# Differential heads: the rotation of queries and keys wholly on GpSimd, their squares on ScalarE, the chain of steps spread over two ticks more

## The chip, the core and the metric

The kernel runs on one core of a Trainium2 chip. Five engines work side by side, each through its own queue in order: TensorE (PE in the profile; its weight loads are PEld), VectorE (DVE), ScalarE (ACT), GpSimd (POOL) and SyncE (SP), which here issues nearly all DMAs. An instruction waits on semaphores for what other engines or DMAs must have done first, and all that stands behind it on its queue waits with it. The metric is the device time of one execution in microseconds (us), lower is better.

## What is computed

A decoder layer for 2048 tokens of width 1024. One input projection feeds two groups of attention heads: eight "stick-breaking" heads and four "differential" heads. The differential part is what this case is about; its queries and keys are normalised per 64-wide map and rotated before the attention:

```
def rmsnorm(x, g, eps=NORM_EPS):
    y = xf * lax.rsqrt(jnp.mean(xf * xf, axis=-1, keepdims=True) + eps) * g
def rope(x, pos):
    x1, x2 = xf[..., :half], xf[..., half:]
    return jnp.concatenate([x1 * cos - x2 * sin, x1 * sin + x2 * cos], axis=-1)
...
dq = rope(rmsnorm(to_pair(d_q), diff_q_norm_g[layer]), pos)
dk = rope(rmsnorm(to_pair(d_k), diff_k_norm_g[layer]), pos)
d_out = differential_attention(dq, dk, dv, lam)      # softmax(q1k1) - lam * softmax(q2k2), times v
d_out = rmsnorm(d_out, diff_subln_g[layer], SUBLN_EPS) * (1.0 - lambda_init)
mix = jnp.concatenate([sb_out, d_out], axis=-1)
x = x + mix @ w_o[layer]
x = x + (jax.nn.silu(h2 @ w_gate) * (h2 @ w_up)) @ w_down      # h2 = rmsnorm(x)
```

## The kernel before

Numbers are kept as pairs of float16 (a high part and the rest), so a product is two or three matmuls. Four stages follow one another: the input norm (to some 85 us), attention in eight groups (0 to 3 stick-breaking, a pair of heads each; 4 to 7 differential, one head each), the rest of the output projection, and the feed-forward part.

The attention of the differential groups is cut into units: 128 queries (one of 16 rows `i`) against up to 1024 keys, for one of the two maps (`units_diff`, L878). A group has 48 units. TensorE makes the scores, VectorE takes their maximum (L917), ScalarE makes a bias of it (L925) and the exponentials (L931); once a row's two maps are there, VectorE subtracts one from the other (`mix`, L965), both halves are split off (L974 to L987), transposed by DMA (L327) and multiplied with the values (`values`, L992). The row's norm takes two GpSimd instructions (L1016, and L108 called from there) and then ScalarE (L1024) and VectorE (L1029).

The program's order is made by a clock of **ticks** (`Ticks`, L33). One unit is one tick; `clock.at(d, fn)` puts a step into the tick that is `d` later. So the tick numbers set only the order in which instructions stand in each engine's queue; there is no time in them. Between units TensorE gets pieces of other work: the projections of the next group's queries, keys and values (`project_diff`, L599; one piece per unit), in the last group the first half of the output projection (`output_sb`, L1062; two pieces per unit). When a group's units are over and pieces are left, they are put out alone, a tick each (L1225; for the last group L1261).

Each differential group has four chunks of 512 tokens, 16 chunks in all. After a chunk's queries and keys are projected into the tile `st` (two buffers, `staged` counts those in use), a **chain** of steps runs over it, started by `begin` (L726); only one chain runs at a time, since the tile `rt` has one buffer and `roping` guards it:

- tick 0: `squares` on GpSimd (L663, 128x1024, from `st` into `rt`); tick 1: `rstd`, sums on VectorE (L667, L669), the power on GpSimd (L108)
- tick 3: `normalise` for queries and for keys, VectorE (L675) and GpSimd (L677); ticks 4 and 5: `rotate`, of each half four products and a difference and a sum
- tick 7: `high`; tick 8: `low`, then `finish` with three DMA transposes from `rt`, `rt` and `st` into `k` and `q` (L712). There `st` and, at once, `roping` are given free.

The next chain writes its squares into `rt`, so it has to wait for the DMAs that read `rt`.

## Time and profile before

| what | us |
|---|---|
| median of three runs | 2873.72 |
| the three runs | 2872.24, 2873.72, 2876.29 |
| the profiled execution, its own time | 2869.62 |
| its span in the profile | 2867.8 |
| TensorE, VectorE, ScalarE, GpSimd busy | 2540.9, 2333.7, 1533.4, 1462.7 |
| mean granted TensorE clock | 0.952 of full speed |

The profiled execution took 4.1 us less than the median, and 1.8 us of its time lie outside the span. The first chain of the differential heads begins at 659.6 us (while the last stick-breaking group still runs), and the last one ends at 1332.4 us; after 1340 us nothing of the changed code runs. Busy time counts an instruction from its start to its end, also where it stands still within that time. The chain that ended last follows the work back from the last instruction and tells which engine and line each moment of the span hung on.

### The profile page before, as it was taken

To read this page: it belongs to the slowest core of one execution; us is meant where nothing else is said; L and a number is where in the kernel's file an instruction comes from. 1 tells how busy PE (TensorE), PEld (TensorE's weight loads), DVE (VectorE), ACT (ScalarE), POOL (GpSimd) and SP (SyncE) were. 2 spreads that over 40 slices of the span, in tenths; PEclk is the share of its full clock that TensorE was granted. 3 is DMA by queue.
4 is the path that set the end of the run, shared out by engine and by line. 5 is a ranking of instruction groups with operands and counts; after the bars stand their busy time and mean duration, and the time that the engine had idled before them with its cause. 6 is when DMAs were issued, how large, how long until landed. Compare 5 with 4: busy or idle time off the path is not lost.

```text
span 2867.8 us, 50589 instructions
## 1 busy us (share of the span) xinstructions
PE 2540.9 (89%) x19628; PEld 1470.6 (51%) x19628; DVE 2333.7 (81%) x3639; ACT 1533.4 (53%) x2587; POOL 1462.7 (51%) x1131
## 2 busy tenths in 40 slices
PE   6978888887786887877998989999999999999999
PEld 4534445455675775765853444444444444444444
DVE  7798998988898898998748789889787767776776
ACT  5788788886555655555426544544443433343332
POOL 1454555547667576774214656654444444444542
PEclk8989999998998999988999999999999999999999
DMA  4576888766554556668765222221217421112111
GB/s 159 91 146 120 144 142 142 135 133 122 100 91 91 97 105 109 136 116 178 167 162 130 88 100 74 74 77 60 88 45 147 153 97 45 45 44 89 45 45 74
DMA packets 734242, 301.57 MB, mean 105 GB/s; under 512 B 618672, under 2 KB 713264, under 8 KB 734000
## 3 DMA queue, kind: packets, MB, share of 16 engines
q1 hardware_dynamic: 733856, 298.30, 46.5%
q8 instruction: 153, 2.51, 0.4%
q14 instruction: 89, 0.73, 0.1%
q0 software_dynamic: 144, 0.03, 0.0%
HBM read 127.34 MB, written 28.31 MB: 54 GB/s over the span
## 4 chain that ended last, share of the span: by engine, by line
PE 43%; DVE 20%; ACT 6%; POOL 5%; DMA 5%; issue 5%; SPq 1%; DVEq 0%; POOLq 0%; ACTq 0%
PE pw L167 33%; PE psum L167 10%; DMA wt<-wh 2%; DVE mx L178 2%; DVE fs L1382 2%; DVE acc_a L1655 2%; DVE pp L178 1%; DVE hh L1434 1%; DVE pp L807 1%; DVE wh L836 1%; DMA q<-rt 1%; DVE wmx L105 1%; DVE rt L683 1%; DVE st L675 1%; ACT pp L802 1%
## 5 line engine op out<-in xcount | busy, mean ns | idle before, releaser
L167 PE MATMUL pw<-t,fs 128*128 128x512 f16 x3696 | 806.5, 380 | 9.6 <-ACT fs L1381 3.8
L167 PEld LDWEIGHTS <-fs 128*128 128x128 f16 x3696 | 360.4, 98 | 447.0 <-issue 9.3
L818 POOL TENSOR_TENSOR pp<-pp 128x1024 f32<-128x1024 f32 (+1 forms) x160 | 325.1, 2032 | 316.2 <-DVE pp L815 139.8
L167 PE MATMUL pw<-acc_b,at 128*128 128x512 f16 x2112 | 467.6, 382 | 17.9 <-DVE cg L1580 8.2
L167 PE MATMUL psum<-k,q 64*128 64x512 f16 (+4 forms) x1600 | 290.3, 378 | 157.9 <-DVE pp L810 77.0
L167 PE MATMUL psum<-ws,h_hi 128*128 128x128 f16 x4096 | 379.0, 225 | 20.6 <-ACT psum L1011 11.4
L167 PE MATMUL psum<-ws,h_lo 128*128 128x128 f16 x2048 | 368.2, 224 | 0.0
L167 PEld LDWEIGHTS <-h_hi 128*128 128x128 f16 x4096 | 329.0, 101 | 49.5 <-issue 38.1
L167 PEld LDWEIGHTS <-at 128*128 128x128 f16 x2112 | 206.9, 98 | 270.8 <-issue 28.3
L1583 POOL TENSOR_TENSOR cg<-cg,cu 128x512 f32<-128x512 f32 x88 | 112.1, 1274 | 360.9 <-ACT cg L1582 341.4
L1655 DVE SCALAR_TENSOR_TENSOR acc_a<-pw,isd,acc_a 128x512 f32<-128x512 f32 x352 | 248.7, 745 | 51.1 <-PE pw L167 50.7
L1381 ACT ACTIVATE fs<-acc_b,fst 128x512 f16<-128x512 f32 x264 | 175.9, 713 | 211.3 <-POOL acc_b L1370 145.2
L1382 DVE SCALAR_TENSOR_TENSOR fs<-acc_b,fst,fs 128x512 f16<-128x512 f32 x264 | 248.6, 982 | 33.1 <-ACT fs L1381 33.0
L1572 POOL TENSOR_TENSOR sc<-sc 128x512 f32<-128x512 f32 x132 | 219.4, 1679 | 88.3 <-ACT sc L1566 88.3
L807 DVE TENSOR_TENSOR_SCAN pp<-pp,psum 128x256 f32<-128x256 f32 (+1 forms) x320 | 195.9, 653 | 56.0 <-ACT psum L804 55.1
L167 PEld LDWEIGHTS <-q 64*128 64x128 f16 (+1 forms) x1600 | 95.6, 99 | 269.6 <-issue 113.4
L1566 ACT COPY sc<-pw 128x512 f32<-128x512 f32 x176 | 100.3, 581 | 209.6 <-PE pw L167 186.1
L167 PEld LDWEIGHTS <-h_lo 128*128 128x128 f16 x2048 | 206.9, 101 | 0.0
L836 DVE TENSOR_TENSOR wh<-pp,wh 128x1024 f16<-128x1024 f32 (+1 forms) x160 | 204.7, 1279 | 0.3 <-DMA wt<-wh 0.3
L931 ACT ACTIVATE pp<-psum,nb,ds_sc 128x1024 f32<-128x1024 f32 (+4 forms) x192 | 183.0, 954 | 22.8 <-DVE pp L178 8.6
L178 DVE TENSOR_REDUCE mx<-psum 128x1 f32<-128x1024 f32 (+4 forms) x192 | 173.7, 905 | 20.3 <-PE psum L167 19.5
L802 ACT ACTIVATE pp<-psum,gsc 128x1024 f32<-128x1024 f32 (+1 forms) x160 | 164.8, 1030 | 34.5 <-PE psum L167 30.5
(224 smaller groups left out, 4545.7 us busy)
## 6 DMA issues: line engine op xcount, KB each, us to landing
acc_b<-in_w_gate_dram SPq DMA_DIRECT2D x22, 1024.0 KB, 5.2
acc_b<-in_w_up_dram SPq DMA_DIRECT2D x22, 1024.0 KB, 7.7
acc_b<-in_w_down_dram SPq DMA_DIRECT2D x22, 1024.0 KB, 9.6
raw<-in_w_in_dram SPq DMA_DIRECT2D x24, 512.0 KB, 4.4
pp<-in_x_dram SPq DMA_DIRECT2D x16, 512.0 KB, 5.3
wt<-wh SPq DMA_TRANSPOSE x512, 3.2
raw<-in_w_o_dram SPq DMA_DIRECT2D x16, 512.0 KB, 4.1
mt<-mix_d SPq DMA_DIRECT2D x32, 256.0 KB, 3.3
```

The costliest lines, as they stand in the source:

```text
L167: nc.tensor.matmul(ps, lhsT=lhsT, rhs=rhs, start=start, stop=stop)
L178: fn(*a, **k)
L802: nc.scalar.activation(be, z[:, :, 0:W], AF.Sigmoid, scale=sc[:, 0:1])
L807: nc.vector.tensor_tensor_scan(ga, ga, z[:, h, P:W][:, ::-1], 2.0 ** 14 if diag else cx[a][:, h, 0:1], ALU.mult, ALU.mult)
L818: nc.gpsimd.tensor_mul(b4, b4, gp[:, :, 1:P + 1].rearrange("p h (r n) -> p h r n", r=1).to_broadcast([128, 2, 2, P]))
L836: nc.vector.tensor_sub(wl[:, 0:n], b2, u["wh"][:, 0:n])
L931: nc.scalar.activation(pt, u["z"][:, 0:e - b], AF.Exp, scale=ds_sc, bias=nb[:, m:m + 1], accum_out=su[:, jj:jj + 1])
L1381: nc.scalar.activation(w[:, m, 0:4], src, AF.Copy, scale=sw)
L1382: nc.vector.scalar_tensor_tensor(w[:, m, 4:8], src, sw, w[:, m, 0:4], ALU.mult, ALU.subtract)
L1572: nc.gpsimd.tensor_add(s[m], s[m], y[m])
L1583: nc.gpsimd.tensor_mul(g, g, u)
L1655: nc.vector.scalar_tensor_tensor(acc[:, i, hs], ps, pr.isd, acc[:, i, hs], ALU.mult, ALU.add)
```

## The change

- `squares` moves from GpSimd (a product of `st` with itself) to ScalarE (its Square function), same tile and size.
- `rotate` has no VectorE instruction any more. Before, of the four products of each half VectorE made two (L683, L684; 128x256) and GpSimd two. Now GpSimd makes all, three instructions instead of four: the two sine products of 128x256, and one cosine product of 128x512 in place of the two of 128x256. The difference and the sum stay on GpSimd.
- `high`, `low` and `finish` stand one tick later, and `roping` is given free two ticks after `finish` instead of in it. A chain can so begin at the earliest eleven ticks after the one before, not eight.

```
-                nc.gpsimd.tensor_mul(r["tmp"]...., x3, x3)
+                nc.scalar.activation(r["tmp"]...., st...., AF.Square)
...
-                nc.gpsimd.tensor_mul(y1, x2, bc(1))
-                nc.vector.tensor_mul(y2, x1, bc(1))
-                nc.vector.tensor_mul(x1, x1, bc(0))
-                nc.gpsimd.tensor_mul(x2, x2, bc(0))
+                x = st[:, t].rearrange("p j m (h f) -> p j (m h) f", h=2)
+                nc.gpsimd.tensor_mul(y1, x2, bc(1, 2))
+                nc.gpsimd.tensor_mul(y2, x1, bc(1, 2))
+                nc.gpsimd.tensor_mul(x, x, bc(0, 4))
                 nc.gpsimd.tensor_sub(x1, x1, y1)
                 nc.gpsimd.tensor_add(x2, x2, y2)
...
                 staged[0] -= 1
-                roping[0] = False
+
+                def over():
+                    roping[0] = False
+
+
+                clock.at(2, over)
...
-                clock.at(7, high)
-                clock.at(8, low)
-                clock.at(8, finish)
+                clock.at(8, high)
+                clock.at(9, low)
+                clock.at(9, finish)
```

Line numbers of the changed kernel are one higher from L667 on and six higher from the end of `finish` on. What it does to the queues, at three places:

VectorE's queue in the first chunk of group 7, from the sums on to the two rotations. `mx` is a unit's maximum, `cf` and `pp` belong to `mix`, `st` and `rt` to the chain. Before:

```order
L675 TENSOR_TENSOR st<-st,qss 128x512 x2
...
L952 TENSOR_SCALAR cf<-cf,su,nlam 128x1
L683 TENSOR_TENSOR rt<-st,cs 128x8x32
L684 TENSOR_TENSOR st<-st,cs 128x8x32
L178 TENSOR_REDUCE mx<-psum 128x1
L919 TENSOR_TENSOR mx<-mx 128x1
L683 TENSOR_TENSOR rt<-st,cs 128x8x32
L684 TENSOR_TENSOR st<-st,cs 128x8x32
L178 SCALAR_TENSOR_TENSOR pp<-pp,cf 128x512
L178 TENSOR_REDUCE mx<-psum 128x1
```

Now:

```order
L676 TENSOR_TENSOR st<-st,qss 128x512 x2
...
L958 TENSOR_SCALAR cf<-cf,su,nlam 128x1
L178 TENSOR_REDUCE mx<-psum 128x1
L925 TENSOR_TENSOR mx<-mx 128x1
L178 SCALAR_TENSOR_TENSOR pp<-pp,cf 128x512
L178 TENSOR_REDUCE mx<-psum 128x1
```

The four products of the chain are gone from between the units' own instructions, which keep their order.

GpSimd's queue in the same chunk, the first of the two rotations with what stands around it; `wh` is the low part of a row's weights, `cf` and `oss` belong to rows' norms. Before:

```order
L677 TENSOR_TENSOR st<-st,qkg 128x512 x2
L985 TENSOR_TENSOR wh<-pp,wh 128x1024
L682 TENSOR_TENSOR rt<-st,cs 128x8x32
L685 TENSOR_TENSOR st<-st,cs 128x8x32
L686 TENSOR_TENSOR st<-st,rt 128x8x32
L687 TENSOR_TENSOR st<-st,rt 128x8x32
L956 TENSOR_SCALAR cf<-su,gsc 128x1
L1016 TENSOR_SCALAR oss<-oss,cf 128x1
L108 TENSOR_TENSOR oss<-oss,mhalf 128x1
```

Now:

```order
L678 TENSOR_TENSOR st<-st,qkg 128x512 x2
L991 TENSOR_TENSOR wh<-pp,wh 128x1024
L684 TENSOR_TENSOR rt<-st,cs 128x8x32
L685 TENSOR_TENSOR rt<-st,cs 128x8x32
L686 TENSOR_TENSOR st<-st,cs 128x512
L687 TENSOR_TENSOR st<-st,rt 128x8x32
L688 TENSOR_TENSOR st<-st,rt 128x8x32
L962 TENSOR_SCALAR cf<-su,gsc 128x1
L1022 TENSOR_SCALAR oss<-oss,cf 128x1
L108 TENSOR_TENSOR oss<-oss,mhalf 128x1
```

One product more stands ahead of the rows' norms, and the cosine product is twice as wide.

ScalarE's queue at the start of group 7, around the group's fourth unit, where the chain of its third chunk now begins; `nb` and `pp,su` are a unit's bias and exponentials. Before:

```order
L526 ACTIVATE ws<-raw,wo_sc 128x1024
L925 ACTIVATE nb<-mx,lnk,nds_sc 128x1
L931 ACTIVATE pp,su<-psum,nb,ds_sc 128x256
L1024 ACTIVATE mxs<-on,oss 128x128
L974 CAST wh<-pp 128x1024
```

Now:

```order
L526 ACTIVATE ws<-raw,wo_sc 128x1024
L663 ACTIVATE rt<-st 128x1024
L931 ACTIVATE nb<-mx,lnk,nds_sc 128x1
L937 ACTIVATE pp,su<-psum,nb,ds_sc 128x256
L1030 ACTIVATE mxs<-on,oss 128x128
L980 CAST wh<-pp 128x1024
```

The squares stand ahead of the unit's bias and exponentials.

TensorE's queue moves a little too. The third chunk of group 4 is projected one unit later, so that two ticks of pieces more are put out alone between groups 3 and 4 (six ticks, before four); between the last scores of group 3 and the first of group 4 stand 48 projection matmuls more. And the output projection of the last group starts one unit later: after the last scores 264 of its matmuls are left, before 240.

## Rows read from the trace of the kernel before

**Rows 1.** The page's part 4: the whole chain that ended last, by line.

```profile
PE pw L167 33%; PE psum L167 10%; DMA wt<-wh 2%; DVE mx L178 2%; DVE fs L1382 2%; DVE acc_a L1655 2%; DVE pp L178 1%; DVE hh L1434 1%; DVE pp L807 1%; DVE wh L836 1%; DMA q<-rt 1%; DVE wmx L105 1%; DVE rt L683 1%; DVE st L675 1%; ACT pp L802 1%
```

**Rows 2.** Two stretches: length, then busy PE, PEld, DVE, ACT, POOL, clock, DMA share, GB/s.

```profile
660.00:1340.00 680.00, 517.68 (x6579) 429.41 (x6577) 608.39 (x1010) 382.61 (x880) 463.79 (x434) 0.89 0.60 110
1340.00:1460.00 120.00, 114.11 (x1114) 95.68 (x1114) 79.04 (x143) 49.37 (x104) 24.32 (x29) 1.00 0.78 174
```

**Rows 3.** Sums over 16 chains (L663 to L718), and 16 rotations alone (L683 to L687).

```profile
sum 511.40, PE 374.47 PEld 310.25 DVE 475.18 ACT 284.90 POOL 405.31; mean PE 23.40 PEld 19.39 DVE 29.70 ACT 17.81 POOL 25.33
...
sum 165.00, PE 120.42 PEld 101.43 DVE 162.66 ACT 83.40 POOL 157.44; mean PE 7.53 PEld 6.34 DVE 10.17 ACT 5.21 POOL 9.84
```

**Rows 4.** VectorE's groups, 660 to 1340 us: count | busy us, mean ns | idle before.

```profile
L683 DVE TENSOR_TENSOR rt<-st,cs 128x256 f32<-128x256 f32 x32 | 27.5, 858 | 2.3 <-POOL st L677 2.3
L684 DVE TENSOR_TENSOR st<-st,cs 128x256 f32<-128x256 f32 x32 | 26.6, 832 | 1.1
```

**Rows 5.** Single lines on VectorE: duration in ns, least/median/most, first and last start.

```profile
L683 DVE TENSOR_TENSOR rt<-st,cs x32: 409/417/2404, 677.9 to 1319.9; 128x256 f32<-128x256 f32 x32
...
L684 DVE TENSOR_TENSOR st<-st,cs x32: 424/830/2239, 678.3 to 1320.4; 128x256 f32<-128x256 f32 x32
...
L644 DVE SCALAR_TENSOR_TENSOR v<-psum,v x32: 424/424/426, 636.8 to 1296.4; 128x256 f16<-128x256 f32 x32
```

**Rows 6.** GpSimd's groups, 660 to 1340 us.

```profile
L677 POOL TENSOR_TENSOR st<-st,qkg 128x512 f32<-128x512 f32 x32 | 44.9, 1422 | 7.8 <-DVE st L675 7.8
...
L687 POOL TENSOR_TENSOR st<-st,rt 128x256 f32<-128x256 f32 x32 | 34.3, 1071 | 0.0
...
L663 POOL TENSOR_TENSOR rt<-st 128x1024 f32<-128x1024 f32 x16 | 33.4, 2087 | 26.3 <-DMA q<-rt 26.3
L686 POOL TENSOR_TENSOR st<-st,rt 128x256 f32<-128x256 f32 x32 | 30.4, 949 | 1.5 <-DVE st L684 1.5
L685 POOL TENSOR_TENSOR st<-st,cs 128x256 f32<-128x256 f32 x32 | 27.6, 863 | 2.5
L682 POOL TENSOR_TENSOR rt<-st,cs 128x256 f32<-128x256 f32 x32 | 27.1, 847 | 0.0
```

**Rows 7.** ScalarE's groups, 660 to 1340 us.

```profile
L925 ACT ACTIVATE nb<-mx,lnk,nds_sc 128x1 f32<-128x1 f32 x117 | 44.7, 382 | 109.0 <-DVE mx L919 86.9 <-DVE mx L178 21.9
...
L802 ACT ACTIVATE pp<-psum,gsc 128x1024 f32<-128x1024 f32 x14 | 15.6, 1111 | 1.7 <-PE psum L167 1.6
```

**Rows 8.** Who waited for whom, 660 to 1340 us: us in total, times, longest.

```profile
PE psum L167 <- ACT pp L931: 76.8, 54, 5.6
...
POOL rt L663 <- DMA q<-rt: 26.3, 8, 6.4
...
DVE qss L667 <- POOL rt L663: 17.2, 7, 5.5
...
ACT st L627 <- DMA q<-st: 16.4, 4, 5.7
...
ACT mxs L1024 <- POOL oss L108: 8.5, 7, 3.4
```

**Rows 9.** The chain that ended last, 660 to 1340 us, by line (cut where the view cuts).

```profile
by line: PE psum L167 14.6%; issue 11.0%; DVE mx L178 8.1%; DVE pp L178 5.4%; DMA wt<-wh 4.8%; DMA q<-rt 3.3%; DVE rt L683 3.2%; DVE st L675 2.9%; POOL rt L663 2.3%; DVE wh L178 2.3%; POOL wh L985 2.2%; POOL cf L956 1.9%; SPq L712 1.8%; DVE
```

**Rows 10.** GpSimd in order of time at the start of group 6: start, us, instruction [idle before].

```profile
1082.68 0.66 POOL L718 COPY st<-rt 128x512 f16<-128x512 f16 x1 [0.83 <-DVE rt L709]
1087.32 2.35 POOL L663 TENSOR_TENSOR rt<-st 128x1024 f32<-128x1024 f32 x1 [3.98 <-DMA q<-rt]
```

**Rows 11.** The chain's three transposes (L712), from issue to landing.

```profile
DMA to landing us min/median/max: 3.2/3.5/5.2
```

**Rows 12.** The exponentials of all 192 differential units: durations, first and last start.

```profile
L931 ACT ACTIVATE pp<-psum,nb,ds_sc x192: 437/1042/1208, 750.6 to 1422.8; 128x1024 f32<-128x1024 f32 x80, 128x128 f32<-128x128 f32 x16, 128x256 f32<-128x256 f32 x16, 128x384 f32<-128x384 f32 x16
```

**Rows 13.** The stretch between groups 3 and 4, columns as in rows 2.

```profile
725.00:750.00 25.00, 15.39 (x189) 12.97 (x187) 24.02 (x32) 9.41 (x14) 16.17 (x14) 0.86 0.83 141
```

**Rows 14.** TensorE's groups, 1340 to 1460 us: the first half of the output projection.

```profile
L167 PE MATMUL psum<-ws,mt 128*128 128x256 f16 x720 | 82.9, 272 | 4.6 <-DVE acc_a L1101 2.4 <-DVE acc_b L1101 2.1
```

More of the change, by code (lines that the diff above doesn't have):

```diff
@@ L648, in project_diff, with bc @@
             r = {}
-            def bc(n):
+            def bc(n, k):
                 return r["cs"][:, n].rearrange("p j (o f) -> p j o f", o=1).to_broadcast(
-                    [128, 4, 2, 32])
+                    [128, 4, k, 32])
             x3 = st.rearrange("p t j m d -> p (t j m) d")
@@ L662, in squares @@
                 r["tmp"] = r["rt"][:, 0:1024].rearrange("p (t j m d) -> p t j m d", t=2, j=4, m=2)
-                nc.gpsimd.tensor_mul(r["tmp"].rearrange("p t j m d -> p (t j m) d"), x3, x3)
+                nc.scalar.activation(r["tmp"].rearrange("p t j m d -> p (t j m d)"),
+                                     st.rearrange("p t j m d -> p (t j m d)"), AF.Square)
             def rstd():
@@ L674, in normalise @@
                 y = x3[:, 8 * t:8 * t + 8, :]
-                (nc.vector, nc.vector)[t].tensor_mul(y, y, r["ss"][:, 8 * t:8 * t + 8].rearrange(
+                nc.vector.tensor_mul(y, y, r["ss"][:, 8 * t:8 * t + 8].rearrange(
                     "p (a o) -> p a o", o=1).to_broadcast([128, 8, 64]))
```

## The prediction

> **What bounds the kernel now.** I read the chain that ended last first. For 33% of the span it hangs on TensorE's matmuls into `pw`, which are those of the feed-forward part, where none of the changed code runs; only for 10% on those into `psum`, attention and projections [rows 1]. So I went to the stretch from 660 to 1340 us, which holds all 16 chains. There VectorE is busy 608.4 of 680 us (89%), TensorE 517.7 (76%), GpSimd 463.8 (68%) and ScalarE 382.6 (56%); behind it, from 1340 to 1460, TensorE is busy 114.1 of 120 and VectorE 79.0 [rows 2]. The first stretch is VectorE's, the second TensorE's. Inside the chains it is plainer: their 16 stretches sum to 511.4 us with VectorE busy 475.2 (93%), and in the 165.0 us of the rotations alone VectorE is busy 162.7 and GpSimd 157.4: both are full, and each holds the other up [rows 3].
>
> How they hold each other up shows in single instructions. A rotation product on VectorE takes 409 ns at its least and up to 2404; the median of the second is 830, twice its least of 424 [rows 5]. The 64 of them are busy 27.5 + 26.6 = 54.1 us [rows 4], while at their least they would take 32 x 0.409 + 32 x 0.424 = 26.7. So 27.4 us are standing still inside the instruction. An instruction of the same size on VectorE that reads one operand from PSUM takes 424 to 426 ns in all 32 cases [rows 5], though GpSimd runs beside it too. So it is two SBUF operands that meet GpSimd.
>
> The waits tell who is late: ScalarE stood 86.9 us for VectorE's maxima before the bias [rows 7], TensorE 76.8 us for ScalarE's exponentials, which free the score banks [rows 8]. A late VectorE thus reaches TensorE through ScalarE. The chain that ended last goes through the first rotation product for 3.2% of 680 us, 21.8 us, through the second for less than the list's last entry, 1.8%, or 12 us, and through GpSimd's squares for 2.3%, 15.6 us [rows 9].
>
> **The change, part by part.** The sum is made against the profiled execution's own time, 2869.6 us; the median of the runs, 2873.7, is 4.1 higher, and I add that at the end.
>
> *Rotation off VectorE.* Removed are 64 instructions, 54.1 us busy [rows 4]. All of it counts if VectorE is the bound wherever they stand; the 93% busy inside the chains [rows 3] speaks for nearly all. The chain that ended last gives 21.8 us [rows 9] as the least: another path is then next, mostly the maxima, which VectorE reaches sooner. I take the middle, -38 (ends -54 and -22).
>
> *What the other VectorE instructions get for it.* GpSimd's rotation was 27.1 + 27.6 + 30.4 + 34.3 = 119.4 us in 128 instructions [rows 6]. Now it is the two sine products at the first one's 847 ns, 54.2, the wide product at the price of the normalisation, the same size on the same engine, 1422 ns x 32 = 45.5 [rows 6], and the difference and sum as they are, 64.7: together 164.4, or 45.0 more. The first of them can meet VectorE's own two-operand instructions, the row differences and splits. Each removed product stood still for 27.4 / 64 = 0.43 us; if one other instruction per rotation now stands still as long, that is 32 x 0.43 = 14; if VectorE is simply past it, 0. I take +6, nearer the lower end, since 64 instructions that could stand still are gone as well.
>
> *Squares to ScalarE.* GpSimd loses 33.4 us [rows 6]. ScalarE gets 16 instructions; the nearest row is another 128x1024 activation, 1111 ns [rows 7], so 17.8 us. They stand ahead of a unit's bias, where ScalarE idled 109.0 us in all before 117 of them [rows 7]; I count +5 (0 to 18). In return VectorE waited 17.2 us in 7 chains for GpSimd's squares, which themselves waited 26.3 us in 8 for the transposes out of `rt` [rows 8]. Two ticks more between `finish` and the next squares are 7 us: the exponentials of 192 units start from 750.6 to 1422.8, so a tick is 672.2 / 191 = 3.5 us [rows 12]. A transpose lands 3.5 us after its issue [rows 11], so that most of this wait goes. Not at the starts of groups, where the units are small and the ticks short: there the chain of group 6's third chunk already had two ticks, and its squares still waited 3.98 us [rows 10]. Four of the pairs lie so. I take half of 17.2, -9 (0 to -17). And in those four the wait is now ScalarE's, with a unit's bias and exponentials queued behind it, and TensorE behind those: up to 4 x 4.0 = 16, I take +4. Squares together: 0.
>
> *GpSimd later.* Net it has 45.0 - 33.4 = 11.6 us more, but the extra 45.0 / 16 = 2.8 us per chain come in two neighbouring ticks. Behind them in its queue are the rows' norms, for which ScalarE waited only 8.5 us so far [rows 8], and the low parts of the weights, which have three ticks to spare. The tick that `high` moves covers 3.5 us of it, so ScalarE's share of `high` waits no longer than before. Below nothing it can come too, since the squares are gone: the path through them was 15.6 [rows 9], less the 17.8 of ScalarE that stands in for it. I take +6 (-10 to +32, the upper end being 2 us of late norm per rotation).
>
> *The spread.* The next scores need a chunk's keys and queries; `finish` of the third chunk of groups 6 and 7 now stands two ticks before the first scores that use them, and its three transposes follow one another on SyncE's queue and land 3.2 to 5.2 us after their issue [rows 11]. Six ticks covered that before; two short ones may not, at 0 to 4 us for each of the two places: +3. Projections that wait for `st` follow `finish` in six places instead of five; ScalarE stood 16.4 us in 4 of them for that DMA [rows 8], so one more is 0 to 4: +2. Two ticks of projection, 48 matmuls, are put out alone between groups 3 and 4; VectorE is busy 24.0 of 25 us there and TensorE 15.4 [rows 13], so its idle time hides nearly all: +1. At the end, 24 more matmuls of the output projection are left after the last scores, where TensorE is the bound [rows 2]; at 82.9 / 720 = 0.115 us [rows 14] that is +2.8. Together +9.
>
> Sum: -38 + 6 + 0 + 6 + 9 = -17, so 2852.6 on the profiled scale, 2856.7 on the median's. Forecast: **2857 us**.
>
> **The rivals.**
>
> *The standing still only moves.* What goes with the products on VectorE is their own 26.7 us, of which the chain already counts 21.8 [rows 9], while the 27.4 us of standing still pass to the row differences and splits, at the same two engines in the same ticks: -22 + 14 + 0 + 0 + 9 = +1, 2875. For it speaks that both engines are full in the rotations [rows 3], and that GpSimd gets longer; against, that the median unit instruction need not stand beside a rotation. The Trainium skill, "SBUF — State Buffer", section "Who interferes with whom", states the rule behind it: a VectorE instruction with two SBUF inputs contends with a GpSimd instruction that reads SBUF, whoever starts first holds the shared port for its whole length, and a reduction never contends. By that rule the trace's stalls are port waits and pass to any other two-input instruction that starts during a GpSimd one; the steady 424 ns of the PSUM reader agree with it.
>
> *GpSimd becomes the bound and the time is longer.* In the rotations it is busy 157.4 of 165 already [rows 3], and gets 45 us more there. If the backlog exceeds one tick, 3.5 us, the rows' norms come after the tick in which ScalarE reads them, ScalarE stops in front of L1024 with exponentials behind it, and TensorE's score banks come free late. That decides once it costs over 23 us; at its upper end, 32 in place of 6, the sum is -38 + 6 + 0 + 32 + 9 = +9: 2883. Against it: averaged over the chains GpSimd is busy 405.3 of 511.4 [rows 3], so that two ticks are enough to catch up.
>
> *VectorE is the bound throughout.* Then all 54 us count, the wait for squares goes wholly (-17), ScalarE's squares lie in its idle time, and only the other VectorE instructions' 6 and the spread's 9 are paid: -54 + 6 - 17 + 6 + 9 = -50, 2824. For it: 93% [rows 3]. Against: the path through these products was 22 us, and TensorE has 374 us of work in those 511.
>
> **How the numbers follow.** Forecast 0.58, its own range 2841 to 2873, from the ends of the rotation's term; the stalls only move 0.18; GpSimd the bound 0.15; VectorE the bound throughout 0.09. A difference of 0.2%, 5.7 us, is about the least that a measurement of this kernel can tell. Faster by more than that, under 2868.0: the forecast and the last rival, 0.67, less 0.06 for the forecast's upper edge, plus 0.02 of the first rival: 0.63. Slower, over 2879.4: the second rival and the upper part of the first, 0.17. Within: 0.20. The range leaves about one in ten out on each side: from between the last rival and the forecast, 2829, to past the second rival's time, 2885.
>
> **What would show it.** In the changed profile between 660 and 1340 us: VectorE's busy time down by 40 to 50 us and its remaining two-operand instructions' means up by a few per cent at most (if by a quarter in the rotations, the first rival holds); the squares on ScalarE at 1.1 us, with a wait for a DMA before them only at the starts of groups; ScalarE's wait for L108's result at 8 to 20 us (over 40: the second rival); GpSimd's rotation at some 164 us; and the last stretch with TensorE over 95% busy and some 3 us longer. The prediction is wrong if the stretch ends no earlier while VectorE is less busy: then the work hung on something that I put second, the exponentials, the banks or the transposes.

## The result, and the profile after

| kernel | median, us | runs |
|---|---|---|
| before, beside it | 2872.98 | 2870.35 to 2876.29 |
| after | 2889.36 | 2888.74 to 2893.22 |

The ratio is 1.0065, 95% interval [1.0053, 1.0077]: of 2872 us that is +18.7 (15.2 to 22.1), slower, where 2857 was forecast and the range ended at 2885. In this part every difference is such a ratio times 2872; the expectations quoted below used differences of medians (+16.4 for the change), which lie up to 3.4 us off.

The profiled execution after has a span of 2887.0 us, 19 more than before. The stretches, columns as in [rows 2]: first the one of before, then one that ends where the last chain ends now, then the last.

```profile
660.00:1340.00 680.00, 509.49 (x6561) 422.44 (x6559) 568.25 (x934) 391.65 (x882) 458.05 (x434) 0.88 0.59 108
...
660.00:1355.00 695.00, 518.27 (x6619) 428.83 (x6617) 578.80 (x950) 400.22 (x901) 471.50 (x450) 0.88 0.59 108
1355.00:1480.00 125.00, 117.38 (x1139) 98.20 (x1139) 80.28 (x147) 49.14 (x104) 25.81 (x31) 1.00 0.78 171
```

In the same 680 us VectorE works 568.25 instead of 608.39 [rows 2], 40.1 less, and TensorE 8.2 less: VectorE has become less busy and the work has become slower. The rotations show it at a glance, as in [rows 3] (L684 to L688 now):

```profile
sum 178.64, PE 126.64 PEld 101.16 DVE 149.86 ACT 88.94 POOL 172.89; mean PE 7.91 PEld 6.32 DVE 9.37 ACT 5.56 POOL 10.81
```

None of the rotation's instructions is VectorE's any more, and in these stretches it fell from 99% to 84% busy; but they take 178.6 us instead of 165.0, and GpSimd is busy in 172.9 of them, 97%. The groups of GpSimd and ScalarE, 660 to 1355 us:

```profile
L686 POOL TENSOR_TENSOR st<-st,cs 128x512 f32<-128x512 f32 x32 | 46.5, 1454 | 2.5
...
L687 POOL TENSOR_TENSOR st<-st,rt 128x256 f32<-128x256 f32 x32 | 31.2, 976 | 2.5
L684 POOL TENSOR_TENSOR rt<-st,cs 128x256 f32<-128x256 f32 x32 | 31.1, 971 | 0.0
L685 POOL TENSOR_TENSOR rt<-st,cs 128x256 f32<-128x256 f32 x32 | 26.9, 840 | 0.0
L688 POOL TENSOR_TENSOR st<-st,rt 128x256 f32<-128x256 f32 x32 | 26.0, 812 | 0.0
...
L663 ACT ACTIVATE rt<-st 128x1024 f32<-128x1024 f32 x16 | 16.8, 1048 | 4.4 <-DMA q<-rt 4.4
```

The rotation is 161.7 us on GpSimd and the squares 1.05 us each on ScalarE; both prices had been put right (164.4 and 1.11). What had not is who waits (before in [rows 8]):

```profile
PE psum L167 <- ACT pp L937: 91.7, 46, 8.4
...
DVE mxs L1035 <- ACT mxs L1030: 39.5, 18, 5.7
...
ACT mxs L1030 <- POOL oss L108: 23.7, 12, 4.6
...
ACT st L627 <- DMA q<-st: 21.5, 6, 5.7
ACT rt L705 <- POOL st L688: 21.5, 6, 8.8
```

L1030, where ScalarE reads a row's norm, waited 8.5 us for GpSimd and now 23.7; TensorE waits 91.7 instead of 76.8 for the exponentials that free its banks. VectorE's wait behind L1030, 39.5 us now, was 9.7 before, too small for the rows shown there.

### The profile page after: what moved, and what is told of

It is laid out like the page before. It is cut to its first block, busy times and chain, and to the rows that moved or that the text cites. A ratio compares the mean times of both kernels' runs of the same rounds, so it can differ in the third digit from the quotient of the medians.

```text
span 2887.0 us, 50525 instructions
## 1 busy us (share of the span) xinstructions
PE 2544.6 (88%) x19628; PEld 1471.0 (51%) x19628; DVE 2303.0 (80%) x3575; ACT 1548.0 (54%) x2603; POOL 1468.7 (51%) x1147
## 4 chain that ended last, share of the span: by engine, by line
PE 36%; DVE 9%; POOL 4%; ACT 3%; DMA 3%; issue 2%; SPq 0%; DVEq 0%; ACTq 0%; POOLq 0%
PE pw L167 33%; PE psum L167 3%; DVE acc_a L1661 2%; DVE fs L1388 2%; DVE hh L1440 1%; DMA wt<-wh 1%; POOL sc L1578 1%; DVE wmx L105 1%; DVE at L1594 0%; ACT fs L1387 0%; DVE fmx L105 0%; DVE cg L1586 0%; ACT pw L1430 0%; POOL hn L1426 0%; DMA t<-hh 0%
## 5 line engine op out<-in xcount | busy, mean ns | idle before, releaser
L167 PE MATMUL psum<-k,q 64*128 64x512 f16 (+4 forms) x1600 | 295.1, 383 | 176.9 <-ACT pp L937 91.7
L167 PEld LDWEIGHTS <-h_hi 128*128 128x128 f16 x4096 | 330.2, 101 | 42.4 <-issue 31.1
L937 ACT ACTIVATE pp<-psum,nb,ds_sc 128x1024 f32<-128x1024 f32 (+4 forms) x192 | 182.7, 952 | 25.0 <-POOL wh L991 12.4
```

What stands on the lines that cost most here:

```text
L167: nc.tensor.matmul(ps, lhsT=lhsT, rhs=rhs, start=start, stop=stop)
L937: nc.scalar.activation(pt, u["z"][:, 0:e - b], AF.Exp, scale=ds_sc, bias=nb[:, m:m + 1], accum_out=su[:, jj:jj + 1])
```

## The experiments

In the names of the runs, *rotation*, *squares* and *spread* are the three parts of the change. All ratios are against the kernel before, run beside them; each difference has some 3 to 4 us either way, by its interval. The edits are shown shortened, several statements to a line. Line numbers differ from run to run by a few; the tiles tell which step it is.

| kernel | ratio | interval | us of 2872 |
|---|---|---|---|
| the change | 1.0065 | 1.0053, 1.0077 | +18.7 |
| rotation | 1.0101 | 1.0087, 1.0114 | +29.0 |
| squares | 1.0068 | 1.0055, 1.0080 | +19.5 |
| spread | 1.0033 | 1.0020, 1.0046 | +9.5 |
| rotation, squares | 1.0157 | 1.0143, 1.0171 | +45.1 |
| rotation, spread | 1.0031 | 1.0020, 1.0043 | +8.9 |
| squares, spread | 1.0039 | 1.0027, 1.0052 | +11.2 |
| before, no VectorE products | 0.9951 | 0.9937, 0.9965 | -14.1 |
| spread, no VectorE products | 0.9944 | 0.9932, 0.9957 | -16.1 |
| spread, rotation on both engines | 1.0119 | 1.0106, 1.0133 | +34.2 |
| change, rotation over four ticks | 1.0059 | 1.0045, 1.0072 | +16.9 |
| third chunk late | 1.0005 | 0.9996, 1.0014 | +1.4 |
| spread in groups 4, 5 | 0.9977 | 0.9966, 0.9988 | -6.6 |
| change, third chunk early | 1.0044 | 1.0031, 1.0056 | +12.6 |
| spread, third chunk early | 1.0002 | 0.9993, 1.0011 | +0.6 |
| release alone in groups 4, 5 | 0.9985 | 0.9975, 0.9995 | -4.3 |
| rotation, spread, norm read later | 1.0008 | 0.9999, 1.0017 | +2.3 |
| spread, norm read later | 1.0044 | 1.0029, 1.0058 | +12.6 |
| rotation, third early, norm later | 1.0009 | 1.0000, 1.0018 | +2.6 |

**The parts alone and in pairs.** The first kernel has rotation and squares without the spread (shown against the change):

```
-                clock.at(2, over)        # roping is given free in finish
-                clock.at(8, high); clock.at(9, low); clock.at(9, finish)
+                clock.at(7, high); clock.at(8, low); clock.at(8, finish)
```

> The change without its spread: squares on ScalarE and the rotation wholly on GpSimd, but the chain's ticks as they were (7, 8, 8) and the next chain let in by the last step. Theory A (GpSimd comes late: its longer rotation pushes the rows' norms back, ScalarE and VectorE stop at L1024 and L1029): still slower than before, +10 to +25 us, at least as slow as the change, with VectorE's wait at L1029 for ScalarE at 30 us or more. Theory B (the spread costs: two ticks of projection put out alone between groups 3 and 4, late keys, a later tail): the loss goes, -15 to +3 us against before.

The spread by itself, on the kernel before:

```
-                roping[0] = False
+                clock.at(2, over)
...
-                clock.at(7, high); clock.at(8, low); clock.at(8, finish)
+                clock.at(8, high); clock.at(9, low); clock.at(9, finish)
```

> The kernel before with only the spread: high, low and finish one tick later, the next chain let in two ticks after the last step. Theory A: within -3 to +5 us of before, since GpSimd has no more to do. Theory B: +8 to +16 us, most of the change's +16, with group 4 beginning some 5 us later and the last stretch some 4 us longer.

The rotation by itself (its lines of the diff, no others):

```
-                nc.vector.tensor_mul(y2, x1, bc(1)); nc.vector.tensor_mul(x1, x1, bc(0))
+                nc.gpsimd.tensor_mul(y2, x1, bc(1, 2)); nc.gpsimd.tensor_mul(x, x, bc(0, 4))
```

> The kernel before with only the rotation moved: five GpSimd instructions for each half and none on VectorE; squares on GpSimd, ticks as before. Theory A: the worst of all, +15 to +30 us, since GpSimd keeps the squares as well (33 us) and has 45 us more. Theory B: a gain, -5 to -20 us, since VectorE is rid of 54 us.

The squares by themselves, and each of the two with the spread:

```
-                nc.gpsimd.tensor_mul(r["tmp"]...., x3, x3)
+                nc.scalar.activation(r["tmp"]...., st...., AF.Square)
```

> The kernel before with only the squares on ScalarE, ticks as before. Without the spread the squares have to wait for the transposes out of rt, now on ScalarE, with exponentials queued behind them (48 us of such waits in the run without the spread). Theory C (the place of the wait counts: what stood on GpSimd for nothing now stops ScalarE): +8 to +20 us, as much as the squares added to the moved rotation (45 - 29 = 16). Theory D (the squares cost nothing by themselves, only a rotation that ends late makes their wait long): -3 to +5 us.

> The kernel before with the rotation on GpSimd and the spread, squares still on GpSimd (33 us more work there than in the change). If GpSimd's load is what is left of the loss: slower than the change, +22 to +35 us against before, with ScalarE's wait at high for GpSimd over 30 us. If the squares on ScalarE are the loss: +5 to +14 us, less than the change's +17.

> The kernel before with the squares on ScalarE and the spread; the rotation as it was, shared by VectorE and GpSimd. If the rotation on GpSimd is what costs (theory A): this loses only the spread's 9 us or less, 0 to +9, and the rows' norms come in time (ScalarE's wait at L1024 for GpSimd under 10 us). If the spread and the squares are the loss and the rotation's move a gain: +17 to +30 us, slower than the change.

Measured: each part alone makes the kernel slower, and rotation and squares together by 45.1 us; the spread takes 26.4 of these off again, though it costs 9.5 alone. So the spread is not what makes the change slow. What it repairs is seen in the waits of the run without it:

```profile
ACT rt L705 <- POOL st L688: 68.8, 15, 8.3
...
DVE rt L704 <- POOL st L687: 48.2, 15, 6.6
ACT rt L663 <- DMA q<-rt: 48.1, 8, 9.6
```

`high` (L704, L705) stands in a queue before GpSimd is through with the longer rotation, and the squares on ScalarE stand before the transposes have read `rt`; in the change these waits are 21.5, 7.9 and 4.4. Theory A's own mechanism was not the main one here: VectorE's wait behind the row's norm is 16.3 us in this run, not 30, and the loss of 45.1 is far over its 25. Of the pairs with the spread, rotation and spread came out as the second case had it, +5 to +14; squares and spread (+11.2) lies between the ranges of both cases, with ScalarE's wait for the norm at 5.3. With the spread the rotation is worth nothing, 8.9 - 9.5 = -0.6, where I had counted on more than 20.

**What VectorE's part is worth, and what GpSimd's costs.** Of VectorE's 64 products nothing is left, and nothing takes their place; the queries and keys are then only partly rotated. First on the kernel before, later on the spread:

```
-                nc.vector.tensor_mul(y2, x1, bc(1))
-                nc.vector.tensor_mul(x1, x1, bc(0))
```

> The kernel before without VectorE's 64 rotation products, which nobody takes over (a sine and a cosine product of each half are left out, so queries and keys are wrong); all else as before. It tells what VectorE's part of the rotation was worth. If VectorE bounds the stretch, as the prediction has it: -22 to -54 us. If the two late engines only hand the time on (the maxima, the exponentials and the score banks are next): -10 us or less.

> The spread, and VectorE's 64 rotation products left out (the queries and keys are then not fully rotated); GpSimd as before. Against the kernel before. Theory V (VectorE's part is worth as much with the spread as without, 13.9 us, and GpSimd's longer rotation takes it back): 9.2 - 13.9 = -5, between -8 and -2. Rival N (with the spread VectorE's products lie beside other waits and are worth nothing; GpSimd's part is free): +6 to +10, like the spread alone.

And the other side: with the spread, GpSimd makes the whole rotation and VectorE two products of the same size besides, into a place that GpSimd then overwrites.

```
+                nc.vector.tensor_mul(y2, x1, bc(1, 2))
+                nc.vector.tensor_mul(y2, x1, bc(0, 2))
                 nc.gpsimd.tensor_mul(y1, x2, bc(1, 2))
```

> The spread, GpSimd's rotation as in the change, and VectorE's two products of each half besides (both written where GpSimd then writes its own, so that they are pure load). So against the spread alone (+9.2) it is GpSimd's longer rotation by itself. Against the kernel before. Theory V (GpSimd's 45 us more cost some 15): +20 to +30. Rival N (GpSimd's part is free): +8 to +13.

Measured: the products cost 14.1 us without the spread and 9.5 + 16.1 = 25.6 with it. GpSimd's longer rotation costs 34.2 - 9.5 = 24.7 in the last run, and 8.9 + 16.1 = 25.0 by the difference of rotation with spread to spread without products: two ways to the same number, 25. It cancels the gain. Without the spread it is 29.0 + 14.1 = 43. Both runs went past theory V's numbers in its own direction (-5 and +20 to +30 expected), since with the spread the products and GpSimd's longer rotation are worth some 25 each, where I had taken 13.9 and 15; the rival that both are free falls. Each of the two 25s has some 5 us either way. ScalarE's wait for the norm in three runs, first the spread without products, then with GpSimd's rotation in place of them, and with both engines' work:

```profile
ACT mxs L1026 <- POOL oss L108: 11.4, 9, 2.1
```

```profile
DVE mxs L1033 <- ACT mxs L1028: 33.3, 18, 4.8
...
ACT mxs L1028 <- POOL oss L108: 27.9, 14, 4.6
```

```profile
ACT mxs L1030 <- POOL oss L108: 14.9, 9, 4.1
```

In the first of them 4.5 us more were spent on the norm's other GpSimd instruction (L1018), so that it is 15.9 there, and 27.9 with GpSimd's rotation. In the spread alone it is 6.0, against 14.9 with both engines' work (to 1355 us). The longer rotation thus adds 9 to 12 us of this wait. At TensorE, the wait for the exponentials that free its banks is 24.5 us longer with it, here in the spread without products, then with GpSimd's rotation in place of them:

```profile
PE psum L167 <- ACT pp L933: 63.1, 41, 5.8
```

```profile
PE psum L167 <- ACT pp L935: 87.6, 44, 8.4
```

**Is it the burst?** The change, with the ten GpSimd instructions over four ticks instead of two:

```
-                clock.at(4, lambda: rotate(0)); clock.at(5, lambda: rotate(1))
+                for d, t, part in ((4, 0, 0), (5, 0, 1), (5, 0, 2), (6, 1, 0), (6, 1, 1), (7, 1, 2)):
+                    clock.at(d, lambda t=t, part=part: rotate(t, part))
```

> The change with the same ten GpSimd instructions of the rotation laid over four ticks (4 to 7) instead of two (4 and 5), so that rows' norms can slip in between; nothing else moves. If the bunch delays the norms (ScalarE and VectorE stopping at L1024 and L1029 for 24 and 40 us): faster than the change by 5 to 12 us, these waits halved. If it is GpSimd's sum of work, or high coming late: the same or slower, -2 to +10 us against the change, with ScalarE's wait at high for GpSimd up from 21 us to 35 or more.

+16.9 against +18.7, within the intervals. The waits, VectorE's and ScalarE's for the norm and both engines' at `high`:

```profile
ACT rt L708 <- POOL st L691: 44.5, 13, 9.7
...
DVE mxs L1038 <- ACT mxs L1033: 24.9, 15, 5.4
DVE rt L707 <- POOL st L690: 22.3, 8, 5.6
...
ACT mxs L1033 <- POOL oss L108: 9.0, 6, 5.0
```

ScalarE's wait for the norm went from 23.7 to 9.0 us and VectorE's behind it from 39.5 to 24.9, as the first case wanted; but `high` now waits 44.5 us on ScalarE instead of 21.5, and 22.3 on VectorE instead of 7.9, as the second had it. So laying the work out brings the norms in time and makes `high` late, and nothing is gained; that the burst itself costs nothing is not shown by it.

**Is it the late norm?** On rotation and spread, both steps that read it stand one tick later; the control has the same on the spread alone.

```
-                    clock.at(10 + n, store_high, "hi")
-                    clock.at(11 + n, store, "")
+                    more = 0 if i == NT - 1 else 1
+                    clock.at(10 + n + more, store_high, "hi")
+                    clock.at(11 + n + more, store, "ev" if more else "")
```

> The rotation on GpSimd and the spread, without the squares (+10.0 by themselves), and in addition the two steps that read a row's norm, on ScalarE (L1024) and on VectorE (L1029), one tick later; the last row of a group keeps its ticks. GpSimd's and VectorE's work is the same. Against the kernel before. Theory M (late norms are most of the 25 us that GpSimd's longer rotation costs): -3 to +2, and ScalarE's wait for L108 under 10 us where it was 27.9. Rival X (the price is VectorE standing still and everything later by that): +7 to +11, although that wait has shrunk.

> The control: the same later reading of the norm on the spread alone, which has VectorE's products and GpSimd's shorter rotation (+9.2 by itself). ScalarE waits only 6.0 us for L108 there. Theory M: +5 to +9, so that this gains far less than with the rotation on GpSimd. Rival X: the same change against its own base as in the other run, within 3 us.

Measured: +2.3 instead of +8.9 with the rotation on GpSimd, +12.6 instead of +9.5 without (expected +5 to +9: the later norm is no gain there, perhaps a loss). So the rotation is now worth 12.6 - 2.3 = 10.3, where it was worth 0.6: late norms are some 10 of the 25 us (the four intervals leave about 7 either way). Rival X falls, since the later norm is worth -6.6 on rotation and spread and +3.1 on the spread alone, not the same within 3. But theory M's "most of the 25 us" is more than this shows. The waits of the first of the two:

```profile
ACT rt L704 <- POOL st L687: 30.9, 12, 10.0
...
ACT mxs L1029 <- DMA mix_d<-mxs: 13.0, 4, 6.7
DVE rt L703 <- POOL st L686: 12.4, 8, 3.7
...
ACT mxs L1029 <- POOL oss L108: 2.7, 4, 0.9
```

The norm's wait is gone (27.9 to 2.7); `high` waits more in its place, 30.9 where rotation and spread had 18.2, and ScalarE now also waits for the DMA that empties `mxs`.

**Where the spread costs.** The exponentials of each unit, set against the same unit of the kernel before, fall behind by 4 to 10 us at one place in group 6 and one in group 7, in every run with the full spread: between the ninth and the seventeenth unit, where the first scores need the third chunk. So I made that chunk alone late, on the kernel before; in a second kernel I kept the spread out of groups 6 and 7; and in a third I turned the change's third chunk earlier.

```
-            clock.at(2, begin)
+            clock.at(6 if c == 2 and g >= 6 else 2, begin)
```

> The kernel before with one thing late: the chain of the third chunk of groups 6 and 7 begins four ticks later, so that its keys and queries are turned at the thirteenth unit of the group instead of the ninth, as they are in the change. No other chain moves. Theory K (late keys: the scores of the ninth row, two units further on, stop TensorE while the transposes are on their way, and the exponentials and rows' norms behind them come late): +10 to +16 us against the kernel before, in two jumps of 5 to 8 us, at the ninth row of groups 6 and 7. Rival P (my prediction's term, the landing time of a transpose less two ticks): +3 us in all. If it is under +5, the jumps seen in the change have another cause, the shift of the other chains.

```
+                wide = 1 if g < 6 else 0
+                clock.at(2 if g < 6 else 0, over)
+                clock.at(7 + wide, high); clock.at(8 + wide, low); clock.at(8 + wide, finish)
```

> The kernel before with the spread for the chains of groups 4 and 5 alone; those of groups 6 and 7 keep their ticks, and the third chunk's keys are turned at the ninth unit there. Theory K: the spread itself is worth something (its lag against the kernel before fell by some 11 us in groups 4 and 5 in the run of the spread alone, before the two jumps), so -6 to -11 us, faster than the kernel before. Rival P (the spread costs by its later release, wherever it stands): +3 to +8 us.

```
+                clock.at(0 if g >= 6 and c < 2 else 2, over)
+                wide = 0 if g >= 6 and c in (1, 2) else 1
+                clock.at(7 + wide, high); clock.at(8 + wide, low); clock.at(8 + wide, finish)
```

> The change, but in groups 6 and 7 the chains of the first three chunks follow one another without the two ticks between, and the last two of these have the old distance of their last steps, so that the third chunk's keys are turned at the ninth unit instead of the thirteenth. All else as in the change. Theory K (late keys cost the change some 13 us): +1 to +6 us against the kernel before, where the change has +16. Rival P (late keys are 3 us): +12 to +15. Theory W (four chains without the spread pay the waits for high and for the squares again, at some 45 - 16 = 29 us for 16 chains, or 7 for four, and late keys are 3): +18 to +22.

My theory K fell with the first: late keys alone cost 1.4 us (-1.1 to 4.0), though the exponentials do fall back by 6 us between the ninth and the seventeenth unit of either group, near K's jumps. Units before that place come sooner, 5.9 us ahead of the kernel before in group 6, because the chain is not yet in their way, and give the gain back there. The change with an early third chunk is at +12.6, in rival P's range and far from K's 1 to 6: what the early chunk gains there, its four chains without the spread mostly pay. The profiled execution shows it: in group 6 the lag no longer grows between those units (8.7 us at the ninth, 8.5 at the seventeenth), but it grows by 6.5 us at the first unit of the group, by 1.5 in the change. But K's second number came in: with the spread in groups 4 and 5 alone the kernel is faster than before, -6.6 (-9.8 to -3.4). So the same spread costs 16.1 us (some 5 either way) in groups 6 and 7. ScalarE in the run of the spread alone, where group 6 starts, in order of time:

```profile
1085.66 0.19 ACT L935 ACTIVATION_READ_ACCUMULATOR pp<-psum,nb,ds_sc 128x1 f32 x1
1091.69 0.38 ACT L627 ACTIVATE st<-psum 128x256 f32<-128x256 f32 x1 [5.83 <-DMA q<-st]
1091.97 0.38 ACT L929 ACTIVATE nb<-mx,lnk,nds_sc 128x1 f32<-128x1 f32 x1
1092.38 0.57 ACT L935 ACTIVATE pp<-psum,nb,ds_sc 128x256 f32<-128x256 f32 x1
1092.84 0.19 ACT L935 ACTIVATION_READ_ACCUMULATOR pp<-psum,nb,ds_sc 128x1 f32 x1
1092.94 0.39 ACT L1028 ACTIVATE mxs<-on,oss 128x128 f16<-128x128 f32 x1
```

SyncE and VectorE beside it:

```profile
1085.16 1.25 SPq L712 DMA_TRANSPOSE k<-rt  x1
1086.52 1.27 SPq L712 DMA_TRANSPOSE q<-rt  x1
1088.23 1.24 SPq L712 DMA_TRANSPOSE q<-st  x1
```

```profile
1093.36 0.35 DVE L1033 SCALAR_TENSOR_TENSOR mxs<-on,oss,mxs 128x128 f16<-128x128 f32 x1 [4.91 <-ACT mxs L1028]
```

The second chunk's `finish` has slipped over the group's start. The next projection is to be put into the `st` that its third transpose still reads; ScalarE stands 5.83 us in front of that, with a bias, an exponential and a row's output behind it, and VectorE stands 4.91 us behind the latter. In the kernel before the same evacuation (L627) starts in this place without a wait:

```profile
1092.36 0.37 ACT L627 ACTIVATE st<-psum 128x256 f32<-128x256 f32 x1
```

At the third chunk, in the spread alone again, TensorE stands first 2.29 us, in which its weight load waits for the second of the chunk's three transposes, then 0.98 us for the third:

```profile
1127.48 0.10 PEld L167 LDWEIGHTS <-q 128*128 128x128 f16 x1 [2.46 <-DMA q<-rt]
1127.49 0.39 PE L167 MATMUL psum<-k,q 128*128 128x512 f16 x1 [2.29 <-ACT pp L935]
...
1128.86 1.46 PE L167 MATMUL psum<-k,q 128*128 128x512 f16 x3 [0.98 <-DMA q<-st]
```

To tell the two apart: the spread, but with the third chunk at once behind the second and with its old ticks, so that only the second slips. And half of the spread in groups 4 and 5, without later ticks.

```
+                clock.at(2 if g < 6 or c == 0 else 0, over)
+                wide = 1 if g < 6 or c < 2 else 0
```

> The spread in groups 4 and 5, and in groups 6 and 7 for the chains of the first two chunks; the chain of the third follows the second's at once and has its old ticks, so that its keys are turned at the eleventh unit, four before the scores that use them. The fourth chunk's as before. So the second chunk's last steps fall into the first two units of the group, as in the change, but the third is not late. Against the kernel before, where the spread in groups 4 and 5 alone gave -6.6 and the full spread +9.2. Theory T (the second chunk's transposes out of st stop ScalarE at the next evacuation while a group starts; 5.8 us at the start of group 6 in the run of the spread alone): 0 to +4, with that wait of 5 to 6 us seen. Rival L (it needs the late third chunk): -7 to -4.

```
+                clock.at(2 if g < 6 else 0, over)      # high, low, finish at 7, 8, 8 as before
```

> The kernel before with half of the spread in groups 4 and 5: the guard is given free two ticks after the last step, and the ticks of that step itself stay as they were; groups 6 and 7 as before. Against the kernel before. If the gain of the spread in groups 4 and 5 (-6.6) is that of squares which no longer wait on GpSimd for the transposes (10.4 us less in the two chains where the gain lies): -5 to -9, and perhaps a little better since no step is later. If it is that the last steps stand a tick further from the rotation: -2 to +2.

+0.6: against -6.6 the second chunk's slip costs 7.2 us (some 4 either way), as theory T had it, and its wait is there:

```profile
1091.35 0.38 ACT L627 ACTIVATE st<-psum 128x256 f32<-128x256 f32 x1 [4.95 <-DMA q<-st]
```

In this kernel the third chunk is also turned two units later than with the spread in groups 4 and 5 alone, and its profiled execution loses part of the 7.2 us only there, so that not all of it is shown to be the second chunk's. The third and fourth chunks' shift on top of it costs the other 8.9 (some 5 either way). Alone, a late third chunk cost 1.4; in these runs it was dear only behind a late second. The release alone brings -4.3 (-7.2 to -1.4) in groups 4 and 5, between the 5 to 9 expected and the 2 at most of the other case; the interval reaches into both. The squares' wait for `rt` in the two chains where the gain lies, before, with the spread in groups 4 and 5, and with the release alone:

```profile
POOL rt L663 <- DMA q<-rt: 10.4, 2, 6.4
```

```profile
POOL rt L663 <- DMA q<-rt: 0.9, 1, 0.9
```

```profile
POOL rt L663 <- DMA q<-rt: 6.3, 1, 6.3
```

With the release alone one of the two chains still waits 6.3 us. So the shorter wait of the squares goes with the gain, but neither that it is the whole of it nor what the later ticks bring is shown.

**Do the repairs add up?** Rotation on GpSimd (its lines as above), squares left there, the third chunk early, the norm read later:

```
+                clock.at(2 if g < 6 or c == 0 else 0, over)
+                wide = 1 if g < 6 or c < 2 else 0
+                    clock.at(10 + n + more, store_high, "hi")
```

> The rotation wholly on GpSimd, the squares left there too; the spread, but with the third chunk of groups 6 and 7 at once behind the second and with its old ticks (this took 8.6 us off the spread alone: +0.6 against +9.2); and the row's norm read one tick later (this took 7.7 off rotation and spread: +2.3 against +10.0). If the terms add: 10.0 - 8.6 - 7.7 = -6, between -9 and -3 against the kernel before, and so about as good as the spread in groups 4 and 5 alone (-6.6). If the early third chunk pays the waits at high again, or hides behind the same waits as the later norm: 0 to +4.

They do not: +2.6 (0.0 to 5.2), no better than with the later norm alone. `high` waits instead, on both engines:

```profile
ACT rt L704 <- POOL st L687: 39.3, 12, 8.7
...
DVE rt L703 <- POOL st L686: 19.9, 8, 4.2
```

With the later norm alone these were 30.9 and 12.4. The increase lies in the chains of the third and fourth chunks of groups 6 and 7, whose last steps stand a tick nearer to their rotation: on ScalarE they wait 19.4 us, where they waited 8.6.

Of the kernels that compute the whole layer, the fastest keep the rotation and the squares where they were: the spread in groups 4 and 5 has ratio 0.9977, and the release alone there, 0.9985, is not to be told from it.

## Why the prediction was wrong, step by step

With the parts put on in the order spread, rotation, squares, the sum can be set against the measurements term by term. It was -17; measured is +18.7. Each measured term but the first is a difference of two ratios, with some 5 us either way.

| term | predicted | measured |
|---|---|---|
| spread | +9 | +9.5 |
| VectorE's products gone | -38 (-54 to -22) | -25.6 |
| others blocked more, GpSimd later | +6 and +6 (-10 to +46 together) | +25.0 |
| squares to ScalarE | 0 | +9.8 |

Of the 35.7 us between the two sums, 12.4 lie in the products, 13.0 in what GpSimd does to others, 9.8 in the squares and 0.5 in the spread. No one of them turned the sign alone: had any one come out as forecast, the change would still have cost 6 us or more.

*What bounds the kernel.* That VectorE bounds the chains was read from its 93% and 99% busy [rows 3]. The reading was too simple: in the rotations GpSimd was at 95% too, and an engine that is full beside another full one is not worth its whole time. The first step that failed is "All of it counts if VectorE is the bound", from which came the middle of 54 and 22, 38. Measured are 25.6 with the spread and 14.1 without, the latter less than the least that I allowed; the 21.8 that the chain through the first product gave [rows 9] lies between them and was the nearest row.

*GpSimd later, and others blocked more.* The second step that failed: 12 us were priced and 25.0 measured. Its instructions were right to 2%, and both mechanisms were named, but each was priced at its lower part: two ticks were thought enough to catch up. Of the 25 us some 10 are norms that ScalarE reads too late, the second rival's mechanism, shown by giving them a tick. Nor does ScalarE's share of `high` wait "no longer than before": it waited 16.6 us before and 21.5 in the change. The spread alone had brought that down to 4.5, and GpSimd's rotation brought it up to 18.2 again. How much of the 25 this is, no run shows by itself, since each repair of the norm made `high` later.

*The standing still.* The first rival's mechanism can be read from the traces. The row differences of the full width, before, in the change, and in the spread without products:

```profile
L178 DVE SCALAR_TENSOR_TENSOR pp<-pp,cf 128x1024 f32<-128x1024 f32 x32 | 46.9, 1464 | 0.0
```

```profile
L178 DVE SCALAR_TENSOR_TENSOR pp<-pp,cf 128x1024 f32<-128x1024 f32 x32 | 50.2, 1569 | 0.0
```

```profile
L178 DVE SCALAR_TENSOR_TENSOR pp<-pp,cf 128x1024 f32<-128x1024 f32 x34 | 50.9, 1496 | 0.0
```

They are 7% longer in the change; but the spread alone already has 1538 ns, so this group decides nothing. Taken over all VectorE instructions but the products, from 660 us to the end of the last chain, the time above the least of the same form is 92 us before and 110 after. With the products left out and nothing put on GpSimd it is 106 on the kernel before, and on the spread it goes from 85 to 103; GpSimd's rotation then makes it 116, with the squares still there. So of the 27.4 us that the products stood still, 14 to 18 passed to other instructions as soon as the products were gone, which the first rival had priced at 14 and my sum at 6. In the table they lie within the -25.6, since no GpSimd instruction had become longer there; the longer rotation added some 14 more (one profiled execution of each). In the rotations themselves the remaining two-operand instructions took 1.43 times their least before and 1.65 now, a sixth more, between my few per cent and the rival's quarter. So the first rival was right on the traces, and the second on the waits; neither decides alone, and my three cases were not exclusive. The rule cited with the first rival, from the Trainium skill, "SBUF — State Buffer", section "Who interferes with whom", agrees with these rows.

*Squares.* The parts were near: VectorE's wait of 17.2 us went wholly (I took 9), the DMA wait is 4.4 us in two places (I took 4). Without the spread the squares waited 42.4 us for the transposes on ScalarE, which is why they cost 19.5 alone. With it they cost 1.7 on the spread and 9.8 on rotation and spread; of ScalarE's 16.8 us I had counted 5. The 9 of gain were counted here, but the spread alone already brings VectorE's wait from 17.2 down to 9.6, so that in the table's order little of it is left for the squares. Where the rest of the 9.8 is lost, no run shows.

*Spread.* The sum was right by chance. A gain of 6.6 in groups 4 and 5 does not stand in it, and in groups 6 and 7 the terms were too small: late keys +3 where the third and fourth chunks cost 8.9, the wait for `st` +2 where the second costs up to 7.2. Of the latter I had priced one more wait by the mean of those seen [rows 8]; in the spread alone there are four more, 26.4 us instead of 16.4, and what they held up, at a place where a unit takes some 3 us, I did not follow. The tail was right: from the last exponentials to the end it was 1445.0 us [rows 12], and is 1448.8 now, by this row and the span.

```profile
L937 ACT ACTIVATE pp<-psum,nb,ds_sc x192: 438/1042/1206, 756.2 to 1438.2; 128x1024 f32<-128x1024 f32 x80, 128x128 f32<-128x128 f32 x16, 128x256 f32<-128x256 f32 x16, 128x384 f32<-128x384 f32 x16
```

*What would show it.* VectorE's busy time fell by the 40 us named, the squares and GpSimd's rotation have the durations named. ScalarE's wait for L108 came out at 23.7, between the 20 that confirmed and the 40 that refuted: a sign that allowed both was no test. TensorE is busy 94% of the last stretch, a little under the 95 named. The last sentence of the prediction is what happened: the stretch ends no earlier while VectorE is less busy.

*Slips in the working.* The sum of the third rival has a 6 for GpSimd that its sentence does not pay; without it that case is 2818, not 2824. The lower end of GpSimd's term, -10, is not worked out: the two numbers beside it, 15.6 and 17.8, give about nothing. Its upper end of 32 counts the two halves of a chain as one rotation, where the standing still counts 32 of them. None of these touches the forecast.

## What to carry to other kernels

Where two engines are both full in a stretch, moving work from one to the other is worth the gain of the one minus the price of the other, and each is to be measured by itself: leave the work out on the one, double it on the other. A step that is moved by a few ticks is to be followed over the boundaries of its surroundings, to the queue that will stand behind it there; the same shift gained 6.6 us in two groups and lost 16.1 in two others. And three small repairs that each work alone need not add, since each makes room for the next wait.

## What was not expected of the hardware

A VectorE instruction on one element per partition can stand still for 2 us. The merge of two maxima, and the maxima themselves, in the changed kernel:

```profile
L925 DVE TENSOR_TENSOR mx<-mx x53: 145/160/2071, 801.0 to 1349.4; 128x1 f32<-128x1 f32 x53
```

```profile
L178 DVE TENSOR_REDUCE mx<-psum x171: 277/947/1226, 754.1 to 1352.3; 128x1 f32<-128x1024 f32 x68, 128x1 f32<-128x128 f32 x16, 128x1 f32<-128x256 f32 x16, 128x1 f32<-128x384 f32 x15
```

The merge reads two operands from SBUF; the 53 take 20.0 us busy where 53 x 0.145 = 7.7 would do. Each of the 14 that took over 300 ns began while a GpSimd instruction on `st`, `rt` or `wh` was running, and ended 14 to 21 ns after the end of that instruction, in one case of the next; merges beside GpSimd's power on a few elements (L108) took 160 ns. It is not the change that does it: before, nine merges were over 300 ns, up to 2075. The maximum reads PSUM and stays within 30 ns for each size, 1197 to 1226 for 1024 elements. ScalarE waited 72.4 us for those merges to end; their standing still is at most 12.3 of it, but it comes in a few large pieces in front of a bias.
